# Attention on one Trainium2 core, summed by parts over differences of the values

## The chip, the cores and the metric

The kernel runs on one core of one Trainium2 chip. The metric is the device time of one execution in microseconds (us). Before the change it is 1481.43 us, the median of three runs (1478.18 to 1483.52). The profile describes a further execution, which took 1480.27 us.

## The reference

One decoder layer with three token mixers that read the same normalised input of 2048 tokens by 1024 columns. One combined projection feeds all three; their outputs are gated, joined and pass through one output projection. The change touches mixer C, stick-breaking attention with 6 heads of 64, for blocks of 128 queries:

```python
z = jnp.einsum('bthd,bshd->bhts', qb, kb) * scale
strict = s_idx[None, :] < t_idx[:, None]
log_not = jnp.where(strict, log_sigmoid(-z), 0.0)
suffix = lax.cumsum(log_not, axis=3, reverse=True) - log_not
a = jnp.where(strict, jnp.exp(log_sigmoid(z) + suffix), 0.0)
out = jnp.einsum('bhts,bshd->bthd', a, vb)
```

With b = sigmoid(z), the weight of key s is b(s) times the product of (1 - b) over all later allowed keys. Write S(s) for the product of (1 - b) over the keys s and later, a masked key counting 1. Then the weight is S(s+1) - S(s), and the sum over keys can be summed by parts: it is the last value row plus the sum over s of S(s) times (v(s-1) - v(s)), with v(-1) = 0.

## The kernel before, in words

Tokens stand in 16 tiles of 128, and these in three blocks of 5, 5 and 6 tiles (`BLOCKS`). Each block goes through three passes p = 0, 1, 2 of two heads each. A pass projects Q, K and V of its tiles (`c_proj`, and `c_evac` for what follows each tile's matmuls), then runs the attention (`stick`). While `stick` runs, `interleave` weaves in matmuls of the other projections as filler: three weight groups in passes 0 and 1, one in pass 2. After the third block a last part, from about 1213 us on, does the mLSTM and the output projection.

**Projection.** A group of weights fills 8 tiles of the pool `wr`, which holds 11. In block 0 the weights come from the input (`load_w`, line 168, into two `st` buffers), ScalarE casts them (line 189), VectorE or GpSimd takes the rest (line 190), and a store keeps both halves in DRAM (line 193); later blocks load those (line 183). In `c_evac`, ScalarE squares Q and K, VectorE sums (line 331), GpSimd takes the power -1/2 (lines 332 and 333), ScalarE and VectorE split V into a high and a low half in `Vst` (lines 334 and 335), and VectorE scales Q and K into `qk` (line 338), which TensorE transposes (line 344). Splits of one tile stand in the queues beside this chain.

**Attention.** A unit is one query tile, one head and up to four key tiles. `front` makes z with two matmuls (lines 378, 379), two sigmoids of z on ScalarE (383 into `bb`, 384 into `be`), on the diagonal two masks on GpSimd (386, 388), and a running product over `bb` from right to left on VectorE (391). One more column of `bb` holds 1 (a memset, line 382). Then `be` is multiplied by the shifted product, by VectorE in one unit and by GpSimd in the next:

```python
eng = nc.gpsimd if len(st_count) % 2 else nc.vector
eng.tensor_tensor(be[:, :w], be[:, :w], bb[:, 1:w + 1], ALU.mult)
```

`middle`, one unit later, transposes `be` (406) and splits the result (ScalarE 408, VectorE 409). `back`, another unit later, multiplies by `Vst` (421). `fin` adds the halves (437), copies (439, ScalarE) and stores `y_d` (440).

**Order.** The framework's scheduler decides the order on each engine from priorities (`prio`); each engine, and SyncE's queue (SP), which starts the DMAs, then takes its instructions in that order. A waiting instruction holds up all behind it.

Of the kernel before, what the change touches and what calls it, by code (L numbers as in the profile page):

```python
# [17 lines left out]
P = 128  # L18
# [14 lines left out]
def hybrid_block_kernel(ctx: ExitStack, tc: tile.TileContext, x, c, norm_g, w_ada, b_ada, w_in,  # L33
# [54 lines left out]

    lw = ExitStack()
    stg_p = lw.enter_context(tc.tile_pool(name="stg", bufs=2))  # L90
    wr_p = lw.enter_context(tc.tile_pool(name="wr", bufs=11))


    rs = ExitStack()
# [114 lines left out]
    brow = [stk.tile([P, 512], F32, tag="bb", bufs=4, name=f"brow{n}") for n in range(4)]  # L209
    for n in (2, 0, 3, 1):  # L210
        nc.gpsimd.memset(brow[n], 0.0)
    g_bc = [stk.tile([P, 512], F32, tag="be", bufs=3, name=f"g_bc{n}") for n in range(2)]

    def ada_load(half):
        for n, c0 in enumerate((1024 + 512 * half, 512 * half)):
# [86 lines left out]
    def c_proj(b, t0, nb, p):  # L302
# [17 lines left out]
            prev = nxt  # L320
        run(prev)

    def c_evac(b, t0, p, j, ps):
        i = t0 + j
        if p == 0:
            nc.vector.tensor_tensor(gates[:, :, i, :], ps[:, 384:392].rearrange("p (a h) -> p a h", a=2),
                                    bif_bc, ALU.add)
        sq = tmp.tile([P, 4, 64], F32, tag="sq", bufs=1, name=f"sq{p}_{i}")
        nc.scalar.activation(sq.rearrange("p a d -> p (a d)"), ps[:, 0:256], AF.Square)
        rr = tmp.tile([P, 4], F32, tag="rr", name=f"rr{p}_{i}")  # L330
        nc.vector.tensor_reduce(rr, sq, AX.X, ALU.add)
        nc.gpsimd.tensor_scalar(rr, rr, 1.0 / 64, EPS, ALU.mult, ALU.add)
        nc.gpsimd.tensor_tensor(rr, rr, neghalf[:, 0:4], ALU.pow)
        nc.scalar.copy(Vst[:, i, :, 0:64], ps[:, 256:384].rearrange("p (h d) -> p h d", h=2))
        nc.vector.tensor_tensor(Vst[:, i, :, 64:128], ps[:, 256:384].rearrange("p (h d) -> p h d", h=2),
                                Vst[:, i, :, 0:64].bitcast(F32), ALU.subtract)
# [12 lines left out]
        nc.vector.scalar_tensor_tensor(ks[64:128], pt[64:128, 2:4, :], gk[64:128], ks[64:128].bitcast(F32),  # L349
                                       ALU.mult, ALU.subtract)  # L350
        nc.vector.scalar_tensor_tensor(Qst[:, j, 1], pt[:, 0:2, :], gq, Qst[:, j, 0].bitcast(F32),  # L351
                                       ALU.mult, ALU.subtract)
        if b < len(BLOCKS) - 1:
            nc.sync.dma_start(k_d[p][:, :, i * P:(i + 1) * P], ks.bitcast(F32))
            nc.sync.dma_start(v_d[p][:, i], Vst[:, i].bitcast(F32))

    def stick(p, t0, nb):
        units = []
# [8 lines left out]
        acc = {}  # L367
        outs = {}
        st = {}
        st_count = []  # L370

        def front(u):
            i, j, h, s0, s1 = u
            w = (s1 - s0) * P
            nm = f"{p}_{i}_{h}_{s0}"
            z = pz.tile([P, 512], F32, tag="z", name=f"z{nm}")
            kk = Kst[:, h, s0 * P:s1 * P]
            nc.tensor.matmul(z[:, :w], lhsT=Qst[:, j, 0, h, :], rhs=kk, start=True, stop=False)  # L378
            nc.tensor.matmul(z[:, :w], lhsT=Qst[:, j, 1, h, :], rhs=kk, start=False, stop=True)  # L379
            bb = stk.tile([P, 513], F32, tag="bb", bufs=4, name=f"bb{nm}")  # L380
            be = stk.tile([P, 512], F32, tag="be", bufs=3, name=f"be{nm}")
            nc.gpsimd.memset(bb[:, w:w + 1], 1.0)  # L382
            nc.scalar.activation(bb[:, :w], z[:, :w], AF.Sigmoid, scale=-1.0)  # L383
            nc.scalar.activation(be[:, :w], z[:, :w], AF.Sigmoid)  # L384
            if s1 == i + 1:
                nc.gpsimd.affine_select(out=bb[:, w - P:w], in_=bb[:, w - P:w], pattern=[[-1, P]],  # L386
                                        compare_op=ALU.is_gt, fill=1.0, base=0, channel_multiplier=1)
                nc.gpsimd.affine_select(out=be[:, w - P:w], in_=be[:, w - P:w], pattern=[[-1, P]],
                                        compare_op=ALU.is_gt, fill=0.0, base=0, channel_multiplier=1)
            rev = bb[:, 0:w + 1][:, ::-1]  # L390
# [40 lines left out]
        def fin(u):  # L431
# [612 lines left out]
```

## Time and profile before

| what | value |
|---|---|
| median of three runs | 1481.43 us |
| the profiled execution | 1480.27 us |
| its span, first to last instruction | 1478.5 us |
| TensorE busy (matmuls) | 1400.6 us, 95% |
| VectorE (DVE) busy | 1025.1 us, 69% |
| ScalarE (ACT) busy | 678.1 us, 46% |
| GpSimd (POOL) busy | 647.3 us, 44% |
| mean granted TensorE clock | 0.982 |

Busy shares are averages over stages with different limits. The windows below give the same numbers by stretch: a stretch's length less TensorE's busy time is what TensorE stood idle there.

### The profile page before, as it was taken

How to read it: one execution, taken by the hardware profiler on the slowest of the kernel's cores; microseconds unless marked ns; L12 is line 12 of the kernel's file. 1: busy time of each engine (PE TensorE's matmuls, PEld its weight loads, DVE VectorE, ACT ScalarE, POOL GpSimd, SP SyncE). 2: the span in 40 equal slices, each digit the busy share in tenths (PEclk: the TensorE clock that was granted, in tenths of full speed). 3: DMA queues.
4: the chain of work that ended last, by engine and by line, in shares of the span. 5: the costliest groups of instructions: out<-in, count | busy, mean ns of one | idle time of the engine just before them, and what ended most of it. 6: DMA issues, size and time to landing. Idle time of an engine off the chain costs nothing.

```text
span 1478.5 us, 24942 instructions
## 1 busy us (share of the span) xinstructions
PE 1400.6 (95%) x8468; PEld 1302.7 (88%) x8468; DVE 1025.1 (69%) x1778; ACT 678.1 (46%) x1656; POOL 647.3 (44%) x1140
## 2 busy tenths in 40 slices
PE   4999999889999999999999899999999978999998
PEld 3789999879999999988899799989999867888887
DVE  6796555586894566588698975778778888444443
ACT  3365444444464355446367655555455655211210
POOL 4463554573443433455233353433344336534442
PEclk9999999999999999999999999999999998999999
DMA  9866766657635534625332343303432524555551
GB/s 319 305 203 216 249 213 190 207 187 240 203 114 194 175 114 137 213 98 184 114 117 78 104 148 131 104 27 107 158 100 74 190 89 128 185 152 159 171 156 57
DMA packets 187103, 233.19 MB, mean 158 GB/s; under 512 B 22714, under 2 KB 160344, under 8 KB 186976
## 3 DMA queue, kind: packets, MB, share of 16 engines
q1 hardware_dynamic: 186752, 231.59, 48.1%
q8 instruction: 67, 1.10, 0.3%
q14 instruction: 60, 0.49, 0.1%
q0 software_dynamic: 224, 0.02, 0.0%
HBM read 159.24 MB, written 72.31 MB: 157 GB/s over the span
## 4 chain that ended last, share of the span: by engine, by line
PE 68%; DVE 16%; DMA 5%; issue 4%; POOL 3%; ACT 3%; SPq 1%; DVEq 0%; POOLq 0%; ACTq 0%
DVE bb L391 6%; PE av L421 5%; PE pc L296 4%; PE pc L298 4%; PE at L406 4%; PE pc L297 4%; PE po L957 4%; PE po L959 3%; PE po L958 3%; PE pg L298 3%; PE pg L297 3%; PE pg L296 3%; PE pb L465 2%; PE pb L464 2%; PE z L378 2%
## 5 line engine op out<-in xcount | busy, mean ns | idle before, releaser
L391 DVE TENSOR_TENSOR_SCAN bb<-bb,bb 128x513 f32<-128x513 f32 x144 | 194.1, 1348 | 24.9 <-ACT bb L383 23.8
L395 POOL TENSOR_TENSOR be<-be,bb 128x512 f32<-128x512 f32 (+3 forms) x120 | 133.0, 1108 | 148.3 <-DVE bb L391 69.2
L409 DVE TENSOR_TENSOR aT<-at,aT 128x512 fp32r<-128x512 f32 (+3 forms) x240 | 142.7, 597 | 31.5 <-ACT aT L408 30.5
L421 PE MATMUL av<-aT,Vst 128*128 128x256 f32 x816 | 146.4, 296 | 15.0 <-DVE aT L409 12.1
L408 ACT CAST aT<-at 128x512 fp32r<-128x512 f32 (+3 forms) x240 | 127.1, 530 | 70.3 <-PE at L406 67.4
L383 ACT ACTIVATE bb<-z 128x512 f32<-128x512 f32 (+3 forms) x240 | 130.3, 544 | 54.5 <-PE z L379 44.2
L421 PEld LDWEIGHTS av<-aT,Vst 128*128 128x128 f32 x816 | 120.5, 192 | 27.0 <-DVE aT L409 19.2
L296 PE MATMUL pc<-wr,hT 128*128 128x384 f32 (+1 forms) x384 | 136.8, 358 | 7.6 <-DVE hT L290 5.7
L406 PE MATMUL at<-ident,be 128*128 128x128 f32 x816 | 132.8, 277 | 9.6 <-DVE Qst L351 4.5
L298 PE MATMUL pc<-wr,hT 128*128 128x384 f32 (+1 forms) x384 | 135.5, 353 | 1.6 <-DVE hT L290 1.5
L297 PE MATMUL pc<-wr,hT 128*128 128x384 f32 (+1 forms) x384 | 134.0, 349 | 0.0
L384 ACT ACTIVATE be<-z 128x512 f32<-128x512 f32 (+3 forms) x240 | 132.1, 550 | 0.0
L406 PEld LDWEIGHTS at<-ident,be 128*128 128x128 f32 x816 | 99.2, 142 | 19.0 <-DVE aT L409 8.0
L957 PE MATMUL po<-wo,yT 128*128 128x512 f32 x256 | 105.0, 410 | 0.3 <-ACT yT L946 0.3
L958 PE MATMUL po<-wo,yT 128*128 128x512 f32 x256 | 102.3, 400 | 1.9 <-DVE wo L864 1.9
L391 DVE TENSOR_TENSOR_SCAN bb<-bb 128x129 f32<-128x129 f32 (+3 forms) x96 | 86.9, 905 | 23.5 <-POOL bb L386 16.3
L959 PE MATMUL po<-wo,yT 128*128 128x512 f32 x256 | 101.5, 400 | 0.0
L382 POOL MEMSET bb<- 128x1 f32 x240 | 24.2, 101 | 168.4 <-DVE bb L391 118.1
L378 PE MATMUL z<-Kst,Qst 128*128 128x512 f32 (+3 forms) x240 | 92.7, 387 | 1.7 <-ACT be L384 1.6
L466 PE MATMUL pb<-hT,wr 128*128 128x320 f32 (+1 forms) x288 | 91.9, 324 | 2.4 <-DVE wr L190 2.4
L464 PE MATMUL pb<-hT,wr 128*128 128x320 f32 (+1 forms) x288 | 93.1, 324 | 0.6 <-DMA wr<-w_d 0.6
L465 PE MATMUL pb<-hT,wr 128*128 128x320 f32 (+1 forms) x288 | 92.2, 322 | 0.0
(272 smaller groups left out, 3905.2 us busy)
## 6 DMA issues: line engine op xcount, KB each, us to landing
wr<-w_d SPq DMA_DIRECT2D x160, 384.0 KB, 5.6
w_d<-wr SPq DMA_DIRECT2D x80, 384.0 KB, 3.5
wad<-in_w_ada_dram SPq DMA_DIRECT2D x8, 1024.0 KB, 6.8
xo<-in_x_dram SPq DMA_DIRECT2D x16, 512.0 KB, 3.7
out_dram<-o SPq DMA_DIRECT2D x31, 256.0 KB, 2.9
xt<-in_x_dram SPq DMA_DIRECT2D x15, 512.0 KB, 3.5
st<-in_w_in_dram SPq DMA_DIRECT2D x60, 128.0 KB, 3.7
wr<-w_d SPq DMA_DIRECT2D x16, 392.0 KB, 6.0
```

The lines of the kernel that those rows point to most:

```text
L296: nc.tensor.matmul(ps, lhsT=hT[:, 0, k, cols], rhs=wt[k][:, 0, :W], start=k == 0, stop=False)
L297: nc.tensor.matmul(ps, lhsT=hT[:, 0, k, cols], rhs=wt[k][:, 1, :W], start=False, stop=False)
L298: nc.tensor.matmul(ps, lhsT=hT[:, 1, k, cols], rhs=wt[k][:, 0, :W], start=False, stop=k == KT - 1)
L384: nc.scalar.activation(be[:, :w], z[:, :w], AF.Sigmoid)
L391: nc.vector.tensor_tensor_scan(rev, rev, rev, carry.get((i, h), 1.0), ALU.mult, ALU.bypass)
L395: eng.tensor_tensor(be[:, :w], be[:, :w], bb[:, 1:w + 1], ALU.mult)
L406: nc.tensor.transpose(at[:, s, :], be[:, s * P:(s + 1) * P], ident)
L409: nc.vector.tensor_tensor(aT[:, :nb_, 1, :], at[:, :nb_, :], aT[:, :nb_, 0, :].bitcast(F32), ALU.subtract)
L421: nc.tensor.matmul(flat(av), lhsT=Vst[:, s0 + s, h, :], rhs=flat(aT[:, s]), start=(s0 + s == i), stop=(s0 + s == 0))
L957: nc.tensor.matmul(po, lhsT=yT[:, 0, k, :], rhs=wo[k][:, 0, cs], start=k == 0, stop=False)
L958: nc.tensor.matmul(po, lhsT=yT[:, 0, k, :], rhs=wo[k][:, 1, cs], start=False, stop=False)
L959: nc.tensor.matmul(po, lhsT=yT[:, 1, k, :], rhs=wo[k][:, 0, cs], start=False, stop=k == KT - 1)
```

## The change

Summation by parts takes the second sigmoid, its mask, the memset and the multiplication out of `front`; `middle` transposes the running product `bb` itself. In exchange `Vst` holds differences v(s-1) - v(s), and `fin` adds the last value row.

For each token tile `c_evac` now copies V out of PSUM (`vt`, line 359), shifts it by one row with a DMA of 127 rows within SBUF (line 360), brings the first row from the tile before (line 357; a memset for the first tile of all) and stores the last row to DRAM (line 361). `values` makes the difference on GpSimd (line 333), its high half on ScalarE (336) and its low half on GpSimd (337), and stores it for later blocks (339). It is called two token tiles later, for the last two tiles of a pass out of `stick`. `stick` loads the last value row, repeated on all partitions (line 416), and VectorE adds it (line 463) where ScalarE copied. In these four places 189 DMAs are added: 45, 48, 48 and 48.

Beside it `bb` gets 6 buffers (4 of `bb` and 3 of `be` before), `wr` gets 13 tiles, and the DMA descriptor scratch of GpSimd is set to 4 KB.

```diff
-    wr_p = lw.enter_context(tc.tile_pool(name="wr", bufs=11))
+    wr_p = lw.enter_context(tc.tile_pool(name="wr", bufs=13))
...
+    def values(pool_after, act_after):
+        b, p, i, dv, vt = late.pop(0)
+        with tc.issue_after(pool_after.ins):
+            nc.gpsimd.tensor_tensor(dv, dv, vt, ALU.subtract)
+        dv2 = dv.rearrange("p (h d) -> p h d", h=2)
+        with tc.issue_after(act_after.ins):
+            nc.scalar.copy(Vst[:, i, :, 0:64], dv2)
+        nc.gpsimd.tensor_tensor(Vst[:, i, :, 64:128], dv2, Vst[:, i, :, 0:64].bitcast(F32), ALU.subtract)
+        if b < len(BLOCKS) - 1:
+            nc.sync.dma_start(v_d[p][:, i], Vst[:, i].bitcast(F32))
...
-        nc.gpsimd.tensor_tensor(rr, rr, neghalf[:, 0:4], ALU.pow)
-        nc.scalar.copy(Vst[:, i, :, 0:64], ps[:, 256:384].rearrange("p (h d) -> p h d", h=2))
-        nc.vector.tensor_tensor(Vst[:, i, :, 64:128], ps[:, 256:384].rearrange("p (h d) -> p h d", h=2),
-                                Vst[:, i, :, 0:64].bitcast(F32), ALU.subtract)
+        rr_pow = nc.gpsimd.tensor_tensor(rr, rr, neghalf[:, 0:4], ALU.pow)
+        dv = tmp.tile([P, P], F32, tag="dv", bufs=4, name=f"dv{p}_{i}")
+        if i == 0:
+            nc.gpsimd.memset(dv[0:1, :], 0.0)
+        else:
+            nc.sync.dma_start(dv[0:1, :], v_before[p][P - 1:P, :])
+        vt = vt_end[:, p, :] if j == BLOCKS[b] - 1 else tmp.tile([P, P], F32, tag="vt", bufs=4, name=f"vt{p}_{i}")
+        v_copy = nc.scalar.copy(vt, ps[:, 256:384])
+        nc.sync.dma_start(dv[1:P, :], vt[0:P - 1, :])
+        nc.sync.dma_start(vl_d[p * NT + i:p * NT + i + 1, :], vt[P - 1:P, :])
+        v_before[p] = vt
+        late.append((b, p, i, dv, vt))
+        if j >= 2:
+            values(rr_pow, v_copy)
...
-            bb = stk.tile([P, 513], F32, tag="bb", bufs=4, name=f"bb{nm}")
-            be = stk.tile([P, 512], F32, tag="be", bufs=3, name=f"be{nm}")
-            nc.gpsimd.memset(bb[:, w:w + 1], 1.0)
-            nc.scalar.activation(bb[:, :w], z[:, :w], AF.Sigmoid, scale=-1.0)
-            nc.scalar.activation(be[:, :w], z[:, :w], AF.Sigmoid)
+            bb = stk.tile([P, 512], F32, tag="bb", bufs=BB, name=f"bb{nm}")
+            front_act[0] = nc.scalar.activation(bb[:, :w], z[:, :w], AF.Sigmoid, scale=-1.0)
...
-                nc.gpsimd.affine_select(out=be[:, w - P:w], in_=be[:, w - P:w], pattern=[[-1, P]],
-                                        compare_op=ALU.is_gt, fill=0.0, base=0, channel_multiplier=1)
-            rev = bb[:, 0:w + 1][:, ::-1]
+                if h == 0:
+                    vlast[i] = stk.tile([P, P], F32, tag="vlast", name=f"vlast{p}_{i}")
+                    nc.sync.dma_start(vlast[i], vl_d[p * NT + i:p * NT + i + 1, :].broadcast_to([P, P]))
+            rev = bb[:, 0:w][:, ::-1]
...
-            eng.tensor_tensor(be[:, :w], be[:, :w], bb[:, 1:w + 1], ALU.mult)
...
-                nc.tensor.transpose(at[:, s, :], be[:, s * P:(s + 1) * P], ident)
+                nc.tensor.transpose(at[:, s, :], bb[:, s * P:(s + 1) * P], ident)
...
-            nc.scalar.copy(yc, py[:, 0:P])
+            nc.vector.tensor_tensor(yc, py[:, 0:P], vlast.pop(i), ALU.add)
...
+            if late and n >= 2:
+                values(front_pool[0], front_act[0])
...
-    nc = _bacc.Bacc("TRN2", target_bir_lowering=False, num_devices=1)
+    nc = _bacc.Bacc("TRN2", target_bir_lowering=False, num_devices=1, dynamic_dma_scratch_size=4096)
```

How the order moves, at three places. First VectorE in the last attention pass (block 2, p = 2), at query tile 15; the running product is printed as SCALAR_TENSOR_TENSOR, and a name holds pass, tile, head and first key tile. Before:

```order
L391 SCALAR_TENSOR_TENSOR bb2_15_0_12_14287<-bb2_15_0_12_14287 128x513
L395 TENSOR_TENSOR be2_15_0_12_14288<-be2_15_0_12_14288,bb2_15_0_12_14287 128x512
L391 SCALAR_TENSOR_TENSOR bb2_15_0_8_14316<-bb2_15_0_8_14316,bb2_15_0_12_14287 128x513
L409 TENSOR_TENSOR aT2_14_1_4_14274<-at2_14_1_4_14269,aT2_14_1_4_14274 128x4x128
L391 SCALAR_TENSOR_TENSOR bb2_15_0_4_14345<-bb2_15_0_4_14345,bb2_15_0_8_14316 128x513
L409 TENSOR_TENSOR aT2_14_1_0_14303<-at2_14_1_0_14298,aT2_14_1_0_14303 128x4x128
L395 TENSOR_TENSOR be2_15_0_4_14346<-be2_15_0_4_14346,bb2_15_0_4_14345 128x512
L391 SCALAR_TENSOR_TENSOR bb2_15_0_0_14394<-bb2_15_0_0_14394,bb2_15_0_4_14345 128x513
```

and of the change:

```order
L418 SCALAR_TENSOR_TENSOR bb2_15_0_12_13688<-bb2_15_0_12_13688 128x512
L433 TENSOR_TENSOR aT2_14_0_0_13609<-at2_14_0_0_13604,aT2_14_0_0_13609 128x4x128
L418 SCALAR_TENSOR_TENSOR bb2_15_0_8_13714<-bb2_15_0_8_13714,bb2_15_0_12_13688 128x512
L433 TENSOR_TENSOR aT2_14_1_12_13629<-at2_14_1_12_13625,aT2_14_1_12_13629 128x3x128
L418 SCALAR_TENSOR_TENSOR bb2_15_0_4_13739<-bb2_15_0_4_13739,bb2_15_0_8_13714 128x512
L451 TENSOR_TENSOR avt2_14_0_13638<-av2_14_0_13544,avs2_14_0_13636 128x128
L433 TENSOR_TENSOR aT2_14_1_8_13654<-at2_14_1_8_13649,aT2_14_1_8_13654 128x4x128
L418 SCALAR_TENSOR_TENSOR bb2_15_0_0_13784<-bb2_15_0_0_13784,bb2_15_0_4_13739 128x512
L433 TENSOR_TENSOR aT2_14_1_4_13675<-at2_14_1_4_13670,aT2_14_1_4_13675 128x4x128
```

The multiplications between the products are gone, and the products run further ahead: those of tile 15 now stand among the splits of tile 14's first head.

Second SP in block 0, at the projection of p = 2; `st10` and `wr10` are that projection's weights, `w_d` the stores. Before:

```order
L168 DMA st10_0_3400<-in_w_in_dram 128x2x128 x3
L440 DMA y_d_63<-yc1_4_3043 128x128
L193 DMA w_d2952_6_3131<-wr9_3_0_3128 256x1x384
L193 DMA w_d2952_7_3136<-wr9_3_1_3133 256x1x384
L193 DMA w_d128_0_3407<-wr10_0_0_3404 256x1x384
L168 DMA st10_1_3414<-in_w_in_dram 128x2x128
L193 DMA w_d128_1_3412<-wr10_0_1_3409 256x1x384
L168 DMA st10_1_3414<-in_w_in_dram 128x2x128 x2
L168 DMA st10_2_3428<-in_w_in_dram 128x2x128 x3
L563 DMA y_d_63<-gu0_0_2782 128x5x64 x2
L355 DMA v_d2_73<-Vst_444 128x256 x2
L193 DMA w_d128_2_3421<-wr10_1_0_3418 256x1x384
```

and of the change:

```order
L171 DMA st10_0_3397<-in_w_in_dram 128x2x128 x2
L171 DMA st10_1_3411<-in_w_in_dram 128x2x128 x3
L464 DMA y_d_63<-yc1_4_3017 128x128
L196 DMA w_d128_0_3404<-wr10_0_0_3401 256x1x384
L360 DMA dv2_0_3143<-vt2_0_3145 127x128
L196 DMA w_d128_1_3409<-wr10_0_1_3406 256x1x384
L196 DMA w_d128_2_3418<-wr10_1_0_3415 256x1x384
L171 DMA st10_2_3425<-in_w_in_dram 128x2x128 x2
L196 DMA w_d128_3_3423<-wr10_1_1_3420 256x1x384
L171 DMA st10_2_3425<-in_w_in_dram 128x2x128
L171 DMA st10_3_3439<-in_w_in_dram 128x2x128 x3
L589 DMA y_d_63<-gu0_0_2765 128x5x64 x2
```

The loads of `st10` follow each other sooner, and the last of them stand ahead of the stores of V and K; the shift of tile 0 (line 360) stands between stores of weights.

Third GpSimd at the same projection (`rr` is the scale of Q and K by tile). Before:

```order
L332 TENSOR_SCALAR rr2_1_3200<-rr2_1_3200 128x4
L333 TENSOR_TENSOR rr2_1_3200<-rr2_1_3200,neghalf_81 128x4
L332 TENSOR_SCALAR rr2_2_3246<-rr2_2_3246 128x4
L333 TENSOR_TENSOR rr2_2_3246<-rr2_2_3246,neghalf_81 128x4
L190 TENSOR_TENSOR wr10_1_1_3423<-st10_1_3414,wr10_1_1_3423 128x384
L332 TENSOR_SCALAR rr2_3_3292<-rr2_3_3292 128x4
L333 TENSOR_TENSOR rr2_3_3292<-rr2_3_3292,neghalf_81 128x4
L190 TENSOR_TENSOR wr10_2_1_3437<-st10_2_3428,wr10_2_1_3437 128x384
```

and of the change:

```order
L350 TENSOR_SCALAR rr2_1_3178<-rr2_1_3178 128x4
L351 TENSOR_TENSOR rr2_1_3178<-rr2_1_3178,neghalf_82 128x4
L350 TENSOR_SCALAR rr2_2_3227<-rr2_2_3227 128x4
L351 TENSOR_TENSOR rr2_2_3227<-rr2_2_3227,neghalf_82 128x4
L333 TENSOR_TENSOR dv2_0_3143<-dv2_0_3143,vt2_0_3145 128x128
L337 TENSOR_TENSOR Vst_446<-dv2_0_3143,Vst_446 128x2x64
L350 TENSOR_SCALAR rr2_3_3280<-rr2_3_3280 128x4
L193 TENSOR_TENSOR wr10_2_1_3434<-st10_2_3425,wr10_2_1_3434 128x384
L351 TENSOR_TENSOR rr2_3_3280<-rr2_3_3280,neghalf_82 128x4
L333 TENSOR_TENSOR dv2_1_3182<-dv2_1_3182,vt2_1_3184 128x128
L193 TENSOR_TENSOR wr10_3_1_3448<-st10_3_3439,wr10_3_1_3448 128x384
L337 TENSOR_TENSOR Vst_446<-dv2_1_3182,Vst_446 128x2x64
```

The difference of tile 0 stands behind the power of tile 2 and ahead of that of tile 3, that of tile 1 directly behind tile 3's.

## Rows read from the trace of the kernel before

**Rows 1.** Page, part 4: chain that ended last, by engine, by line.

```profile
PE 68%; DVE 16%; DMA 5%; issue 4%; POOL 3%; ACT 3%; SPq 1%; DVEq 0%; POOLq 0%; ACTq 0%
DVE bb L391 6%; PE av L421 5%; PE pc L296 4%; PE pc L298 4%; PE at L406 4%; PE pc L297 4%; PE po L957 4%; PE po L959 3%; PE po L958 3%; PE pg L298 3%; PE pg L297 3%; PE pg L296 3%; PE pb L465 2%; PE pb L464 2%; PE z L378 2%
```

**Rows 2.** Windows: length, PE, PEld, DVE, ACT, POOL, clock, DMA share, GB/s.

```profile
0.00:60.00 60.00, 38.08 (x145) 27.04 (x146) 41.35 (x64) 17.71 (x36) 27.42 (x47) 0.91 0.86 300
60.00:120.00 60.00, 57.08 (x387) 54.96 (x386) 52.38 (x102) 36.87 (x100) 34.81 (x69) 1.00 0.73 245
...
240.00:304.00 64.00, 55.21 (x301) 52.45 (x300) 38.09 (x77) 26.29 (x80) 34.77 (x53) 0.91 0.59 184
304.00:420.00 116.00, 112.75 (x711) 107.35 (x710) 92.84 (x174) 58.75 (x155) 54.71 (x107) 0.99 0.66 216
420.00:620.00 200.00, 199.99 (x1254) 193.64 (x1253) 124.54 (x234) 91.61 (x233) 68.87 (x152) 1.00 0.46 151
620.00:712.00 92.00, 82.67 (x509) 78.22 (x508) 78.30 (x119) 51.86 (x130) 55.13 (x95) 0.97 0.43 141
...
810.00:850.00 40.00, 34.48 (x211) 29.99 (x210) 37.49 (x61) 27.16 (x58) 14.97 (x33) 1.00 0.29 96
...
960.00:1050.00 90.00, 87.87 (x562) 83.28 (x561) 74.25 (x120) 48.31 (x118) 33.18 (x72) 1.00 0.25 83
...
1110.00:1175.00 65.00, 63.56 (x406) 59.29 (x404) 51.25 (x81) 40.81 (x97) 24.17 (x61) 1.00 0.29 103
1175.00:1213.00 38.00, 27.38 (x167) 22.60 (x166) 34.60 (x43) 22.48 (x47) 14.63 (x27) 0.91 0.38 137
1213.00:1260.00 47.00, 41.07 (x243) 35.74 (x244) 36.62 (x60) 21.09 (x50) 29.10 (x29) 0.85 0.51 154
...
sum 1478.50, PE 1400.59 PEld 1302.72 DVE 1025.14 ACT 678.15 POOL 647.32; mean PE 87.54 PEld 81.42 DVE 64.07 ACT 42.38 POOL 40.46
```

**Rows 3.** Groups by line and shape: count, busy us, mean ns, idle before.

```profile
L391 DVE TENSOR_TENSOR_SCAN bb<-bb,bb 128x513 f32<-128x513 f32 x144 | 194.1, 1348 | 24.9 <-ACT bb L383 23.8
...
L395 DVE TENSOR_TENSOR be<-be,bb 128x512 f32<-128x512 f32 x66 | 51.1, 774 | 1.3
...
L544 POOL TENSOR_TENSOR gu<-tb 128x128 f32<-128x128 f32 x32 | 20.0, 626 | 29.5 <-DVE tb L543 28.6 <-PE at L406 0.8
...
L335 DVE TENSOR_TENSOR Vst<-pc,Vst 128x128 fp32r<-128x128 f32 x48 | 13.3, 280 | 3.5 <-ACT Vst L334 3.5
...
L384 ACT ACTIVATE be<-z 128x512 f32<-128x512 f32 (+3 forms) x240 | 132.1, 550 | 0.0
```

**Rows 4.** Busy time by stretch, line 395 alone: DVE, then POOL.

```profile
810.00:850.00 40.00, 3.65 (x6) 9.79 (x7) 1.00 0.29 96
...
1175.00:1213.00 38.00, 5.47 (x7) 10.20 (x8) 0.91 0.38 137
...
sum 1478.50, DVE 77.44 POOL 133.01; mean DVE 4.84 POOL 8.31
```

**Rows 5.** Timeline, 626 to 634 us, DVE, POOL: start, length.

```profile
627.13 2.37 DVE L395 TENSOR_TENSOR be<-be,bb 128x256 f32<-128x256 f32 x1
629.42 3.40 DVE L391 TENSOR_TENSOR_SCAN bb<-bb,bb 128x513 f32<-128x513 f32 x1
...
626.46 5.29 POOL L149 TENSOR_TENSOR xt<-xt,hshift 128x1024 f32<-128x1024 f32 x2
```

**Rows 6.** Chain by time, 250 to 304 us: start, length, what.

```profile
264.35 3.42 DMA st<-in_w_in_dram
...
267.87 0.52 ACT wr L189
```

**Rows 7.** SP waits (total, times, longest); DMA issues; line 355.

```profile
SPq L310 <- PE av L421: 44.6, 8, 14.6
...
v_d<-Vst SPq DMA_DIRECT2D x30, 128.0 KB, 3.7
...
L355 SPq DMA_DIRECT2D v_d<-Vst x30: 319/378/1351, 60.4 to 620.2; - x30
```

More of the change, by code (lines that the diff above doesn't have):

```diff
@@ L27 @@
 T5 = 6
+BB = 6
 OFF = dict(au=0, av=256, az=512, bq=768, bk=1152, bv=1536, bo=1920, bz=2304, bi=2688,
@@ L53, in hybrid_block_kernel @@
     v_d = [dram.tile([P, NT, 2, P], F32, name=f"v_d{p}") for p in range(3)]
+    vl_d = dram.tile([3 * NT, P], F32, name="vl_d")
     ident = const.tile([P, P], F32, name="ident")
@@ L75, in hybrid_block_kernel @@
     gates = const.tile([P, 2, NT, 4], F32, name="gates")
+    vt_end = const.tile([P, 3, P], F32, name="vt_end")
     gT = const.tile([P, 64], F32, name="gT")
@@ L208, in hybrid_block_kernel @@
     crow = tmp.tile([8, P], F32, tag="t512", bufs=T5, name="crow")
-    brow = [stk.tile([P, 512], F32, tag="bb", bufs=4, name=f"brow{n}") for n in range(4)]
+    brow = [stk.tile([P, 512], F32, tag="bb", bufs=BB, name=f"brow{n}") for n in range(4)]
     for n in (2, 0, 3, 1):
         nc.gpsimd.memset(brow[n], 0.0)
-    g_bc = [stk.tile([P, 512], F32, tag="be", bufs=3, name=f"g_bc{n}") for n in range(2)]
+    g_bc = [stk.tile([P, 512], F32, tag="bb", bufs=BB, name=f"g_bc{n}") for n in range(2)]
     def ada_load(half):
@@ L321, in c_proj @@
         run(prev)
+    late = []
+    v_before = {}
+    def values(pool_after, act_after):
[8 more added lines that the diff above has]
+            nc.sync.dma_start(v_d[p][:, i], Vst[:, i].bitcast(F32))
     def c_evac(b, t0, p, j, ps):
@@ L354, in c_evac @@
             nc.sync.dma_start(k_d[p][:, :, i * P:(i + 1) * P], ks.bitcast(F32))
-            nc.sync.dma_start(v_d[p][:, i], Vst[:, i].bitcast(F32))
     def stick(p, t0, nb):
@@ L369, in stick @@
         st = {}
-        st_count = []
+        vlast = {}
+        front_act, front_pool = [None], [None]
         def front(u):
@@ L379, in front @@
             nc.tensor.matmul(z[:, :w], lhsT=Qst[:, j, 1, h, :], rhs=kk, start=False, stop=True)
-            bb = stk.tile([P, 513], F32, tag="bb", bufs=4, name=f"bb{nm}")
-            be = stk.tile([P, 512], F32, tag="be", bufs=3, name=f"be{nm}")
-            nc.gpsimd.memset(bb[:, w:w + 1], 1.0)
-            nc.scalar.activation(bb[:, :w], z[:, :w], AF.Sigmoid, scale=-1.0)
-            nc.scalar.activation(be[:, :w], z[:, :w], AF.Sigmoid)
+            bb = stk.tile([P, 512], F32, tag="bb", bufs=BB, name=f"bb{nm}")
+            front_act[0] = nc.scalar.activation(bb[:, :w], z[:, :w], AF.Sigmoid, scale=-1.0)
             if s1 == i + 1:
-                nc.gpsimd.affine_select(out=bb[:, w - P:w], in_=bb[:, w - P:w], pattern=[[-1, P]],
+                front_pool[0] = nc.gpsimd.affine_select(out=bb[:, w - P:w], in_=bb[:, w - P:w], pattern=[[-1, P]],
                                         compare_op=ALU.is_gt, fill=1.0, base=0, channel_multiplier=1)
-                nc.gpsimd.affine_select(out=be[:, w - P:w], in_=be[:, w - P:w], pattern=[[-1, P]],
-                                        compare_op=ALU.is_gt, fill=0.0, base=0, channel_multiplier=1)
-            rev = bb[:, 0:w + 1][:, ::-1]
+                if h == 0:
+                    vlast[i] = stk.tile([P, P], F32, tag="vlast", name=f"vlast{p}_{i}")
+                    nc.sync.dma_start(vlast[i], vl_d[p * NT + i:p * NT + i + 1, :].broadcast_to([P, P]))
+            rev = bb[:, 0:w][:, ::-1]
             nc.vector.tensor_tensor_scan(rev, rev, rev, carry.get((i, h), 1.0), ALU.mult, ALU.bypass)
             carry[i, h] = bb[:, 0:1]
-            eng = nc.gpsimd if len(st_count) % 2 else nc.vector
-            st_count.append(0)
-            eng.tensor_tensor(be[:, :w], be[:, :w], bb[:, 1:w + 1], ALU.mult)
-            st[u] = [be, None]
+            st[u] = [bb, None]
             return 2 * w / 2.4
@@ L401, in middle @@
             nm = f"{p}_{i}_{h}_{s0}"
-            be = st[u][0]
+            bb = st[u][0]
             nb_ = s1 - s0
```

## The prediction

> **What bounds the kernel now.** I read the chain of work that ended last first. TensorE has 68% of it, VectorE 16%, and the running product of line 391 is its longest single line [rows 1]. The change removes no matmul and no transpose, so TensorE's 1400.6 us of work stay [rows 2], and what can be won is the time in which it stands idle or runs at the lower clock. So I cut the span into windows next [rows 2]. Idle is length less TensorE's busy time. From 420 to 620 us it is 0.01 us of 200: there nothing can be won, however much other engines are relieved. Idle worth the name is found in 60 to 120 (2.92), 240 to 304 (8.79), 304 to 420 (3.25), 620 to 712 (9.33), 810 to 850 (5.52), 960 to 1050 (2.13), 1110 to 1175 (1.44) and 1175 to 1213 (10.62): 44.0 us in eight stretches. The start (21.92) and the passage to the last part (5.93) hold no attention that the change touches.
>
> In the same rows the reader sees why. In 810 to 850 VectorE is busy 37.49 of 40 us, in 1175 to 1213 it is 34.60 of 38: there it sets the pace, and line 391 and its followers are its work. In 240 to 304 it is busy only 38.09 of 64, and the chain there runs through a weight load of 3.42 us and the cast behind it [rows 6]: a different cause. [...]
>
> **The change part by part.** ScalarE loses the second sigmoid, 240 of them, 132.1 us at 550 ns [rows 3]. ScalarE paces no stretch (678 us in all [rows 2]), so I count only that each product starts one sigmoid earlier, at nothing: TensorE's filler hides it, and without the filler it would be 0.55 us where a pass begins. GpSimd loses 133.0 us of multiplications, VectorE 77.4 us [rows 4]. The mask and the memset go from GpSimd's queue as well. VectorE's split of V, 13.3 us [rows 3], moves to GpSimd, and 48 additions in `fin` come to VectorE at about the same size, so these two cancel there. GpSimd gains 96 subtractions of 128 by 128; the nearest row has 626 ns [rows 3], 60 us in all, under what it loses. By stretch:
>
> - 1175 to 1213, the last pass. The 5.47 us of multiplications on VectorE fall out of the queue that sets the pace [rows 4]; the order shows products and splits alternating with nothing between. I take 5.5 of the idle 10.62, and half of the clock's 3.4 with it: 7.2. Ends: 0, if TensorE then waits for the products alone, and 14.0.
> - 810 to 850: 3.65 us of multiplications [rows 4], taken whole: 3.7. Ends 0 and 5.52.
> - 960 to 1050 and 1110 to 1175: idle 3.57 together, VectorE busy four fifths of the time [rows 2]. I take 2.5; ends 0 and 3.57.
> - 620 to 712: a multiplication of only 256 columns took 2.37 us and the product behind it 3.40 us, while GpSimd ran two additions of 1024 columns, 5.29 us [rows 5]; the mean product takes 1.35 and a full multiplication 0.77 [rows 3]. The multiplication goes, GpSimd's additions stay. I take 5.0 of the idle 9.33 and the clock's 2.8. Ends 0 and 12.1.
> - 240 to 304: the two more weight tiles let loads of the third projection start sooner, as SP's order shows, but a load still has to land and its split still stands ahead of `qk`. I take 2.5; ends 0 and 14.6 (8.79 and 5.8).
> - 304 to 420: 1.5, ends 0 and 4.5. From 60 to 120: 1.0, ends 0 and 2.9, since there the DMA engines are 73% busy [rows 2] and SP gets 14 more issues.
>
> Sum: 7.2 + 3.7 + 2.5 + 5.0 + 2.5 + 1.5 + 1.0 = 23.4 us. All upper ends give 57.2.
>
> [...]
>
> [...]
>
> Against the gain stand the added waits. 189 DMAs at the 0.378 us that an issue of line 355 takes [rows 7] are 71 us of SP's time over the whole kernel. I cost them at nothing: SP is no compute engine, and between the shift and the difference lie two tiles of projection. One tile is 24 matmuls, at 200 us for 1254 matmuls [rows 2] 3.8 us, so two are 7.7; a 128 KB store of V lands in 3.7 us in the median [rows 7], and the shift moves half of that. The cover is gone where SP holds the shift back: then GpSimd waits at the difference, behind it the power of the next tile, on VectorE `qk`, and TensorE waits for the transposed Q and K. [...]
>
> The sum is made against the profiled execution: 1480.27 - 23.4 = 1456.9 us. The median of the runs is 1.2 us above that execution, so I forecast **1458 us** for the change.
>
> **The rivals.** *Larger gain.* Once VectorE keeps up, the waits at pass starts shrink too, the clock stays up, and products no longer collide. For it: four stretches show both idle and lost clock. Against it: weight and x loads remain. About three quarters of the upper ends, 43 us: 1481.4 - 43 = 1438 us.
>
> *Smaller gain.* Only the stretches that VectorE paces answer: 7.2 + 3.7 + 2.5 = 13.4, so 1468 us. For it: the chain at 264 us runs through a load.
>
> *No change.* TensorE is 95% busy and its waits pass to other work that was nearly as late, the splits (line 409) and the x loads: 1479 us.
>
> *Slower.* SP's queue holds the shifts back. Before, the loads of `Vst` already waited there for the last attention matmul 8 times, 44.6 us in all and 14.6 us at the longest [rows 7], and in later blocks the shifts stand behind such loads. A mean wait of 5.6 plus 3.7 us of landing is 9.3, 1.6 beyond the cover of 7.7; the longest is 18.3, 10.6 beyond. If four of the nine projections meet the longest, that is 42 us, less 23.4 won: 19 us slower, 1500 us. It decides from a mean excess of 28 / 9 = 3.1 us per projection on. Against it: the first differences stand two tiles late, and the wait for attention's last matmul is largely over by the third tile.
>
> *The change doesn't do what it says* would be differences built late enough that `back` waits for `Vst`. The tiles left over are two and are read last, so I give it no chance of its own; it is in the slower case.
>
> **How the numbers follow.** Chances: the forecast 0.42, larger 0.19, smaller 0.16, no change 0.09, slower 0.14. A measurement of this kernel can tell about 0.3%, 4.4 us, from no change: faster is below 1477.0, slower above 1485.9. Faster is 0.42 + 0.19 + 0.16 = 0.77, same 0.09, slower 0.14. The range reaches from 1432, a little past the larger gain (below it lie the all-upper-ends cases near 1424), to 1480, through no change; about 0.05 is left out below and 0.14 above.
>
> **What would show it.** Right: VectorE's total near 948 us (1025 less 77), ScalarE's near 546 (678 less 132), GpSimd's below 575 (647 less 133, and 60 more); the last pass shorter by 7 us, with VectorE no longer ahead of 0.9 busy; line 418 with a smaller share of the chain than line 391; TensorE's busy time within a few us of 1400, and 420 to 620 unchanged but for its place. Wrong: GpSimd waiting in total over 20 us at line 333 for DMAs, `qk` (now line 367) waiting more for GpSimd, and TensorE idle before the transposes of line 373. If idle of the last pass stays near 10 us although VectorE is relieved, the product's own chain was the limit and the sum falls by its largest term. If 240 to 304 and 620 to 712 lose most of their idle, the larger gain is the case.

## The result and the profile after

The change makes the kernel slower: 1514.02 us in the median (1510.92 to 1515.98, 4 runs) against 1481.91 us for the kernel before (1478.18 to 1483.52, 4 runs), a ratio of 1.0223 with a 95% interval of 1.0203 to 1.0243. The forecast was 1458 us, and 1514 lies above the range.

The arithmetic went down as intended, and TensorE did not gain by it. The page of the kernel after, busy time by engine and the chain:

```profile
PE 1412.6 (93%) x8468; PEld 1314.6 (87%) x8468; DVE 941.8 (62%) x1658; ACT 577.9 (38%) x1416; POOL 504.4 (33%) x783
...
PE 61%; DMA 15%; DVE 9%; issue 5%; SPq 4%; ACT 3%; POOL 3%; DVEq 0%; POOLq 0%; ACTq 0%
...
L418 DVE TENSOR_TENSOR_SCAN bb<-bb,bb 128x512 f32<-128x512 f32 x144 | 190.4, 1322 | 14.9 <-ACT bb L410 13.4
```

VectorE lost 83 us, ScalarE 100, GpSimd 143. In the chain VectorE fell from 16% to 9%, but DMA rose from 5% to 15% and SP's queue from 1% to 4% [rows 1]: more of the span now hangs on transfers. The windows show where. Kernel after, columns as in [rows 2]; the last row is the whole middle part, from 60 us to the last attention matmul:

```profile
60.00:120.00 60.00, 53.23 (x332) 50.26 (x331) 39.51 (x78) 29.50 (x82) 27.46 (x51) 0.95 0.69 225
120.00:250.00 130.00, 124.02 (x752) 120.20 (x751) 66.67 (x132) 53.38 (x140) 50.85 (x83) 0.99 0.71 224
250.00:330.00 80.00, 68.70 (x381) 66.00 (x380) 47.25 (x91) 31.80 (x96) 42.48 (x63) 0.94 0.61 186
330.00:380.00 50.00, 45.83 (x283) 43.63 (x282) 30.74 (x68) 20.75 (x55) 19.52 (x30) 0.97 0.59 198
380.00:440.00 60.00, 50.08 (x284) 48.12 (x283) 36.52 (x66) 19.47 (x53) 17.23 (x32) 0.89 0.59 188
...
851.00:891.00 40.00, 38.44 (x247) 36.49 (x246) 32.34 (x56) 21.30 (x45) 2.54 (x8) 1.00 0.29 98
...
1211.00:1249.00 38.00, 31.23 (x206) 26.18 (x205) 32.62 (x43) 20.01 (x41) 4.76 (x5) 0.96 0.65 228
...
60.00:1249.20 1189.20, 1121.95 (x6925) 1073.41 (x6924) 762.36 (x1355) 507.58 (x1258) 356.88 (x615) 0.98 0.48 154
```

The same stretch of the kernel before:

```profile
60.00:1213.40 1153.40, 1108.76 (x6907) 1059.76 (x6906) 848.45 (x1472) 606.72 (x1494) 499.35 (x968) 0.99 0.47 153
```

Length less busy time is TensorE's idle: 44.6 us before, 67.3 after. Its busy time grew by 13.2 us with the same matmuls at a lower mean clock, and 22.6 + 13.2 is the 35.8 us by which the span grew. From 60 to 440 us stand 6.8, 6.0, 11.3, 4.2 and 9.9 us of idle, 38.1 in all; from 60 to 420 us before it was 15.3. The late stretches that VectorE paced did gain: 851 to 891 has 1.6 us idle where 810 to 850 had 5.5, and the last 38 us have 6.8 where they had 10.6. So a gain late is buried under a loss early, at the projections. What the engines waited for there, kernel after (engine, line, what ended the wait: us in total, times, longest):

```profile
ACT wr L192 <- DMA st<-in_w_in_dram: 78.7, 28, 9.1
ACT Vst L336 <- POOL dv L333: 67.4, 25, 8.4
POOL dv L333 <- DMA dv<-vt_end: 36.4, 7, 8.0
POOL dv L333 <- DMA dv<-vt: 13.2, 6, 6.1
...
SPq L312 <- PE z L408: 29.9, 6, 13.4
...
PE z L407 <- ACT bb L410: 15.4, 8, 5.3
```

The first row was 50.9 us (22 times) before; the next three are new. The last row is where TensorE feels them most: its matmuls of z wait for a sigmoid in ScalarE's queue, in four of the eight cases one shortly behind a wait of the first two rows. Before, TensorE waited 1.6 us there. And this is SP's queue of the kernel after at the first shifts (start us, length us):

```profile
63.55 0.73 SPq L360 DMA_DIRECT2D dv<-vt  x1
64.34 3.46 SPq L361 DMA_DIRECT2D vl_d<-vt  x1
67.85 0.62 SPq L357 DMA_DIRECT2D dv<-vt  x1
68.58 0.64 SPq L360 DMA_DIRECT2D dv<-vt  x1
69.27 1.94 SPq L361 DMA_DIRECT2D vl_d<-vt  x1
```

The issue that takes long is the 512 bytes of line 361, right behind the shift of line 360. By tile, kernel after (duration min/median/max in ns):

```profile
L361 SPq DMA_DIRECT2D vl_d<-vt x39: 294/1017/5145, 64.3 to 1125.7; - x39
L361 SPq DMA_DIRECT2D vl_d<-vt_end x9: 1467/2665/4782, 90.9 to 1127.9; - x9
...
L360 SPq DMA_DIRECT2D dv<-vt x39: 625/655/727, 63.6 to 1119.2; - x39
```

Summed over all its issue records, SP spends 601 us on 1012 issues, 417 us on 823 before; 80 us of it are the 48 issues of line 361.

### The profile page after: what moved, and what is told of

It is laid out like the page before. It is cut to its first block, busy times and chain, and to the rows that moved or that the text cites. A ratio compares the mean times of both kernels' runs of the same rounds, so it can differ in the third digit from the quotient of the medians.

```text
span 1514.3 us, 24153 instructions
## 1 busy us (share of the span) xinstructions
PE 1412.6 (93%) x8468; PEld 1314.6 (87%) x8468; DVE 941.8 (62%) x1658; ACT 577.9 (38%) x1416; POOL 504.4 (33%) x783
## 4 chain that ended last, share of the span: by engine, by line
PE 61%; DMA 15%; DVE 9%; issue 5%; SPq 4%; ACT 3%; POOL 3%; DVEq 0%; POOLq 0%; ACTq 0%
PE av L445 5%; PE at L430 4%; DMA st<-in_w_in_dram 4%; PE po L983 4%; PE po L985 4%; PE po L984 4%; PE pc L299 3%; PE pc L300 3%; PE pc L301 3%; DVE bb L418 3%; DMA wr<-w_d 3%; DMA dv<-vt_end 2%; PE z L407 2%; PE z L408 2%; PE pg L299 2%
## 5 line engine op out<-in xcount | busy, mean ns | idle before, releaser
L418 DVE TENSOR_TENSOR_SCAN bb<-bb,bb 128x512 f32<-128x512 f32 x144 | 190.4, 1322 | 14.9 <-ACT bb L410 13.4
L430 PE MATMUL at<-ident,bb 128*128 128x128 f32 x816 | 133.0, 278 | 7.5 <-DVE Qst L380 4.0
L430 PEld LDWEIGHTS at<-ident,bb 128*128 128x128 f32 x816 | 100.7, 143 | 15.9 <-DVE aT L433 4.4
L407 PE MATMUL z<-Kst,Qst 128*128 128x512 f32 (+3 forms) x240 | 93.5, 392 | 15.4 <-ACT bb L410 15.4
L412 POOL TENSOR_SCALAR_AFFINE_SELECT bb<-bb 128x128 f32<-128x128 f32 x96 | 40.4, 422 | 179.5 <-ACT bb L410 149.9
L418 DVE TENSOR_TENSOR_SCAN bb<-bb 128x128 f32<-128x128 f32 (+3 forms) x96 | 83.3, 869 | 25.0 <-POOL bb L412 24.4
L490 PE MATMUL pb<-hT,wr 128*128 128x320 f32 (+1 forms) x288 | 95.5, 332 | 2.6 <-ACT wr L192 2.4
L299 PE MATMUL pa<-wr,hT 128*128 128x384 f32 x256 | 90.3, 353 | 6.9 <-DMA wr<-w_d 4.1
L491 PE MATMUL pb<-hT,wr 128*128 128x320 f32 (+1 forms) x288 | 94.4, 328 | 0.0
L492 PE MATMUL pb<-hT,wr 128*128 128x320 f32 (+1 forms) x288 | 94.4, 330 | 0.0
L299 PE MATMUL pg<-wr,hT 128*128 128x384 f32 x256 | 90.0, 351 | 2.4 <-DMA wr<-w_d 2.4
```

Of the source, the lines that this page charges most:

```text
L299: nc.tensor.matmul(ps, lhsT=hT[:, 0, k, cols], rhs=wt[k][:, 0, :W], start=k == 0, stop=False)
L430: nc.tensor.transpose(at[:, s, :], bb[:, s * P:(s + 1) * P], ident)
```

## The experiments

Three theories. **A**: SP's time for the added issues is the loss. **B**: it is the waiting for the shift's landing, in the order of GpSimd and ScalarE. **C**: the 13 weight tiles. **D** came up after the first four runs and is told there.

**The last value row without its DMAs.** 96 DMAs less; instead of adding the row, 1 is subtracted where the weights are split.

```diff
-        nc.sync.dma_start(vl_d[p * NT + i:p * NT + i + 1, :], vt[P - 1:P, :])
-            nc.scalar.copy(aT[:, :nb_, 0, :], at[:, :nb_, :])
+            nc.scalar.activation(aT[:, :nb_, 0, :], at[:, :nb_, :], AF.Copy, bias=-1.0)
```

> The last value row is no longer stored, loaded and added (96 DMAs less): since the differences telescope, the weights S - 1 give the same sum, and ScalarE and VectorE take the 1 off where they split the transposed product. Theory A (SyncE's queue is filled by the issue of the added DMAs, 159 us of issue time in the profile after, 101 us of it lines 361 and 416, and weight loads behind them come late): most of the 32 us loss comes back, 1485 to 1497 us. Theory B (the engines wait in order for the shift to land): the shift stays, so 1507 to 1515 us. Theory C (the other buffer counts gave a worse order): 1507 to 1515 us.

Measured: 1494.09 us, ratio 1.01 (1.0084 to 1.0117). Some 18 to 20 us come back (by the ratios and by the medians), as A had it. But the long issue only moved to the next in line. Line 357, which now follows the shift of the tile before, takes 66.5 us in 45 issues; in the changed kernel it took 26.7.

**The shifts on ScalarE's queue.** Lines 357, 360 and 361 with `nc.scalar.dma_start`.

> The shift, the first row and the store of the last row (lines 360, 357, 361; 138 us of issue time) are issued by ScalarE, right behind its copy of V, instead of SyncE; the load of the last row stays on SyncE. Theory A: SyncE is as free as before, 1482 to 1495 us, unless ScalarE's 138 us of issuing take the place. Theory B: the landing time is the same, 1505 to 1515 us. Theory C: 1505 to 1515 us.

Measured: 1515.92 us, ratio 1.0245 (1.0229 to 1.0262): nothing gained, though SP's issue time is back at 431 us. That alone does not refute A, which left open that ScalarE's issuing takes the place: ScalarE now spends 135 us on 141 issues. The run has another use: these DMAs now have a queue of their own in the records, q10, beside SP's q1. A stretch in which hardly anything else moves, 199.5 to 202.2 us (DMA busy tenths and GB/s in 40 slices; then packets, MB, share of 16 engines' time by queue):

```profile
DMA  0000000000000000000000000000000000000002
GB/s 23 15 23 23 23 23 23 23 23 23 23 23 23 23 23 23 23 23 23 15 23 23 23 23 23 23 23 15 23 23 23 23 15 23 23 23 23 23 23 91
...
q10 hardware_dynamic: 84, 0.04, 5.2%
q1 hardware_dynamic: 29, 0.02, 2.4%
```

The 23 GB/s are the rate of both queues together, and it hardly changes whether q10 moves alone (12 to 25 GB/s by slices from 93.5 to 94.4 us) or takes turns with q1: one packet of 512 B after the other, about 24 ns apart (113 in 2.7 us). Together the queues take 7.6% of sixteen engines' time here. One sixteenth is 6.25%; the records give a little more because a packet's record, by these rows 27 ns on q10 and 36 on q1, lasts longer than the 24 ns to the next. So 127 packets are 3 us at this pace, while in the first 60 us of the kernel before the DMA engines together move 300 GB/s [rows 2].

The single packets of this stretch show what stands behind the shift. SP had issued a store of V at 196.17 us and one of K at 196.60. Fifteen sixteenths of each, 120 of 128 packets and 240 of 256, had started by 198.5 us. The last 8 of V started between 199.92 and 200.38 us and the last 16 of K between 200.90 and 201.60, each in turn with a packet of the shift, while nothing else moved.

**Without the shift.** Lines 357 and 360 are left out and `dv` is minus `vt`, so the row above is missing from the values; the store and load of the last row stay.

```diff
-        nc.sync.dma_start(dv[1:P, :], vt[0:P - 1, :])
-            nc.gpsimd.tensor_tensor(dv, dv, vt, ALU.subtract)
+            nc.gpsimd.tensor_tensor(dv, vt_zero, vt, ALU.subtract)
```

> The two shift DMAs (lines 360 and 357, 93 of them, 58 us of issue time) are left out and the difference is taken from a tile of zeros, so the attention's values are wrong by the row before; the rest of the change stays. Theory A: about a third of the loss comes back, 1498 to 1506 us. Theory B (waiting for the shift is the loss): nearly all, 1480 to 1492 us. Theory C: 1507 to 1515 us.

Measured: 1451.39 us, ratio 0.9815 (0.98 to 0.983). All of the loss is gone and the gain is there. The run takes away the wait for the landing too, so by itself it tells only that the shift is the cause, not how. The row that tells most is line 362 of this kernel, the same store of 512 B with no shift ahead of it:

```profile
L362 SPq DMA_DIRECT2D vl_d<-vt x39: 215/247/730, 61.1 to 1058.2; - x39
```

247 ns in the median in the place of 1017: the small store was never dear, it was held up by what stood before it.

**11 weight tiles.** `bufs=11` for `wr`, all else as changed.

> The change with 11 weight tiles as before instead of 13. Theories A and B: no better, 1510 to 1525 us, since fewer loads run ahead. Theory C (13 tiles let weight loads stand too early in SyncE's queue and hold up what is behind them): 1480 to 1500 us.

Measured: 1506.46 us, ratio 1.0185 (1.0169 to 1.0201). The two tiles cost 6 to 8 us here (by the ratios and by the medians), so C is a small part at most; the time lies outside the ranges of all three theories.

From these four came **theory D**: the 127 rows run on one DMA engine, and whatever is spread over all engines, the weight loads above all, stands behind them there. It is read from the records of the run on ScalarE's queue: the 23 GB/s in 7.6% of sixteen engines' time, the packets of the two queues in turn, the last sixteenth of each store among them, and the time, 1515.92 us, which the other queue did not change. No record names the engine that moves a packet, so the one engine is the author's estimate from that pace.

**The shift in two pieces**, of 112 and 15 rows.

```diff
-        nc.sync.dma_start(dv[1:P, :], vt[0:P - 1, :])
+        nc.sync.dma_start(dv[1:113, :], vt[0:112, :])
+        nc.sync.dma_start(dv[113:P, :], vt[112:P - 1, :])
```

> Edit: the shift of 127 rows is issued as two, rows 1 to 112 and rows 113 to 127; all else is the changed kernel, and each token tile issues one DMA more (48 more in all). In the run with the shifts on ScalarE's queue, that queue alone moved data from 93.5 to about 96.5 us: 130 packets, 5.7 to 7.0% of sixteen engines' time, at 19 to 25 GB/s, so one packet of 512 B after the other. Theory D: the shift of 127 rows runs on one DMA engine, and what is split over all engines (weights, the next store) waits behind it there; 112 and 15 rows are divided over more engines, so the time falls to 1455 to 1480 us and the mean issue of the last row's store falls from 1.7 us to under 0.6. Theory A (SP's issue time is the loss, whatever the DMA's shape): 48 more issues at about 0.6 us are added to a full queue, 1515 to 1540 us. Theory B (the loss is waiting for a landing in POOL's and ScalarE's order, whatever sets it): falls by what the landing shortens, 1475 to 1505. [...]

Measured: 1465.58 us, ratio 0.99 (0.9881 to 0.992), 48 us less than the changed kernel with 48 issues more. The rows behind it, of this kernel:

```profile
L362 SPq DMA_DIRECT2D vl_d<-vt x39: 253/403/827, 65.6 to 1077.8; - x39
```

D's figures hold: the time, and a mean issue of 0.39 us for the last row's store. A as it was written is refuted, and B's range began 9 us higher. How the 112 and the 15 rows divide over the engines is not shown. One statement in the expectation is not right: q10 was not alone from 93.5 to 96.5 us, where q1 moved 307 packets beside its 119.

**Through DRAM.** The tile's 128 rows are stored one row down and loaded back as 128 rows.

```diff
+        nc.sync.dma_start(vs_d[p, i * P + 1:i * P + P + 1, :], vt)
...
+            nc.sync.dma_start(dv, vs_d[p, i * P:i * P + P, :])
```

> Edit: each tile's 128 value rows are stored to DRAM one row down and loaded back as 128 rows; the row from the tile before and the last row's store fall away, and the last row is read from the same place. About 144 added DMAs in the place of 189, none of them of 127 rows (but for the three first tiles, which keep the shift on the chip, split in 112 and 15). Theory D (127 rows on one DMA engine): both copies are spread, 1455 to 1480 us. Theory A (SP's issue time): 45 issues less, some 90 us of issue less, 1480 to 1500. Theory B (waiting for landings in order): two landings one behind the other in the place of one, 1515 us or more.

Measured: 1460.92 us, ratio 0.9867 (0.9845 to 0.9888). With two landings in series, of 128 rows each, the kernel is faster than with the one of 127 rows (1514.02 us), which B excludes. Its windows and waits:

```profile
60.00:1190.00 1130.00, 1095.26 (x6915) 1052.58 (x6914) 763.15 (x1355) 506.93 (x1258) 360.18 (x615) 1.00 0.51 165
...
1152.00:1190.00 38.00, 31.35 (x216) 26.25 (x215) 32.41 (x44) 20.59 (x42) 6.45 (x5) 1.00 0.65 229
```

```profile
ACT wr L192 <- DMA st<-in_w_in_dram: 62.5, 28, 9.1
ACT Vst L336 <- POOL dv L333: 35.1, 24, 3.8
POOL dv L333 <- DMA dv<-vs_d: 16.3, 10, 5.1
```

Against the kernel before, idle of the middle part is down from 44.6 to 34.7 us and busy time by 13.5, at a clock of 1.00: 23.4 us shorter. The tail takes 2.2 us more; why was not looked into.

**The weight as a difference**, on the kernel before: `be` is the difference of neighbouring elements of `bb`; second sigmoid, mask and product go, no DMA comes.

```diff
-            eng.tensor_tensor(be[:, :w], be[:, :w], bb[:, 1:w + 1], ALU.mult)
+            eng.tensor_tensor(be[:, :w], bb[:, 1:w + 1], bb[:, :w], ALU.subtract)
```

> Edit, on the kernel before: the attention weight is formed as the difference of two neighbouring elements of the scan's output, in the place of the second sigmoid, its mask and the product; values, weight tiles and DMAs stay as before. One 512-wide ScalarE operation and one mask less per unit, no DMA more. If ScalarE's share in the passes is what the changed kernel saves, 1455 to 1472 us; if the saving lies mainly in the product that falls off VectorE and GpSimd, which stays here as a difference, 1472 to 1482 us (no change).

Measured: 1492.88 us, ratio 1.0078 (1.0059 to 1.0097), a miss: slower, though ScalarE does 98 us less. In this kernel the tile's waits read:

```profile
  PE at L403: 79.4, 52
```

In the kernel before the same wait, for the transposes that still read a `be` buffer, was 17.0 us in 3 waits. It seems to have stood in ScalarE's queue and now to stand in those of VectorE and GpSimd, ahead of the next products; that was not tried by itself. Taking the second sigmoid and its mask alone gains nothing.

**No added DMA at all**: the first and the third experiment together, so values are negated in the place of differenced, and the row above is missing from them.

> Edit: the changed kernel without any of the 189 added DMAs: values are negated in the place of differenced, and 1 is subtracted from the weights in the place of adding the last value row. It shows the gain of the change's arithmetic alone. Theory D: the store and load of the last row cost little by themselves (0.28 us an issue where no shift stands before them), so within 8 us of the run without the shifts, 1443 to 1453 us. Theory A: 96 DMAs less again, another 20 us less, 1425 to 1435 us.

Measured: 1450.49 us, ratio 0.9794 (0.9772 to 0.9815). This is the gain of the arithmetic together with the change's buffers, which stay (six of `bb`, 13 weight tiles; not tried apart from it): 29.6 us against the runs of before beside it. It is 0.9 us (by the medians) to 3 us (by the ratios) from the run without shifts that still has the 96 DMAs of the last row: those cost 3 us at most by themselves, and some 18 to 20 us behind a shift.

**127 idle rows on the kernel before.** One more DMA for each token tile into a spare tile that nothing reads, ahead of the store of V.

```diff
+        sp = tmp.tile([P, P], F32, tag="sp", bufs=2, name=f"sp{p}_{i}")
+        nc.sync.dma_start(sp[1:P, :], Vst[0:127, i, 0, :].bitcast(F32))
```

> Edit, on the kernel before: each of the 48 token tiles issues one more DMA, 127 rows of 512 B from the stored values into a spare tile one row down, which nothing reads. No arithmetic changes and nobody waits for it. Theory D (127 rows run on one DMA engine and hold up what is split over all of them): 48 such transfers of about 3.3 us stand in front of weight loads, slower by 15 to 45 us. Theory B (the loss is that GpSimd and ScalarE wait for the landing): 0 to 5 us. Theory A (issue time): 48 issues of 0.65 us, 0 to 8 us, and the same for 128 rows.

Measured: 1514.4 us, ratio 1.0234 (1.0211 to 1.0257). No arithmetic changed, and the kernel is as slow as the changed one. No compute engine waits for these transfers. SP does, for a spare buffer to come free, but only 7.1 us in two waits (2.9 with the 128 rows of the next run).

**128 idle rows**, the control: `sp[0:P]` from `Vst[0:128]`.

> The control of the run with 127 idle rows: the same 48 idle DMAs on the kernel before, of 128 rows (no row shift). Theory D: within 6 us of the kernel before, 1474 to 1486 us. Theory A: as slow as with 127 rows.

Measured: 1481.14 us, ratio 1.0004 (0.9991 to 1.0017). One row more takes the whole loss away. The two runs differ in the offset of one row as well, but the split shift has that offset too and is fast. The store of V that stands behind the idle DMA, by tile, with 127 rows:

```profile
L357 SPq DMA_DIRECT2D v_d<-Vst x30: 415/2222/4291, 62.9 to 646.4; - x30
```

and with 128:

```profile
L357 SPq DMA_DIRECT2D v_d<-Vst x30: 320/587/1229, 62.4 to 621.6; - x30
```

The wait of the weights' cast for its load, with 127 rows:

```profile
ACT wr L189 <- DMA st<-in_w_in_dram: 69.8, 27, 7.9
```

and with 128, where it is about that of the kernel before, 50.9:

```profile
ACT wr L189 <- DMA st<-in_w_in_dram: 52.5, 21, 6.5
```

So both signs of the changed kernel, the long issue behind the shift and the late weights, are there with 127 rows and gone with 128. Summed over all its issues SP spends 528 us with 127 rows and 445 with 128. Theory D stands, its one engine as an estimate; A and B each name only a part. How the 33 us divide between SP's longer issues and the later landings was not separated.

**Through DRAM with 11 weight tiles.**

> Edit: the kernel that carries the values through DRAM, with 11 weight tiles as before the change. In the changed kernel 11 tiles were 8 us faster than 13. If that came from weight loads crowding the one engine that the shifts took, it is gone here: within 4 us of 1461. If 13 tiles cost by themselves, 1450 to 1456 us.

Measured: 1467.24 us, ratio 0.9906 (0.9886 to 0.9926), outside both expectations: 13 tiles are 6 us faster here, where they were 6 to 8 us slower with the shifts. The sign turns with the shifts, though the intervals with and without the two tiles just touch here; that earlier weight loads crowd the one engine is the likely reason, but was argued, not shown.

**Through DRAM, and 1 subtracted from the weights.** The edits of the first and sixth experiment together.

> Edit: the kernel that carries the values through DRAM, and with 1 subtracted from the weights where they are split, in the place of loading and adding the last value row: 48 DMAs less, none of them of an odd shape, and the copy of the output back on ScalarE. Candidate for the fastest. If the 48 loads cost what their issue takes (0.42 us each, in part in the open), 1452 to 1459 us; if spread DMAs are hidden, 1458 to 1464.

Measured: 1459.94 us, ratio 0.9865 (0.9842 to 0.9888), the same as through DRAM alone, 1460.92: the 48 loads of the last row cost nothing here that could be measured. These two versions beat the kernel before by 19 and 22 us, and the changed one by some 53.

## Why the prediction was wrong

**The step that failed** is the one on the added waits: "189 DMAs at the 0.378 us that an issue of line 355 takes ... I cost them at nothing", with "a 128 KB store of V lands in 3.7 us in the median, and the shift moves half of that". It priced the shift by its bytes and by a row of 128 partitions. The 127 rows had another price: on ScalarE's queue they moved at 23 GB/s, with what took turns with them in 7.6% of sixteen engines' time, about that of one engine. With the shift through DRAM or in two pieces the change measured 1461 and 1466 us, near the forecast, in the place of 1514: the term put at nothing was worth about 50 us. The step also counted only what waits for the shift. The 127 idle rows show that such a wait is not needed: 33 us are lost though no compute engine waits for them, while the next issue on SP stands up to 4.3 us and the weights' cast waits 69.8 us for its loads in the place of 52.5.

**The wait at the difference** is likely a second cost. GpSimd waited 49.6 us at line 333, over the 20 us named as a sign of error, and ScalarE 67.4 us behind it (24.7 us without the shifts). The cover of 7.7 us did not suffice where a landing was itself queued: single waits reach 8.0 us. Between the changed kernel and the one with the split shift lie 48 us, more than the 33 of the idle rows. TensorE's wait for the sigmoid, 15.4 us in the changed kernel, is 5.9 with the split shift, 0.6 without the shifts and 4.3 with the idle rows. That fits, but how much of the rest is this wait was not separated.

**The slower rival** had the right sign and place of wait ("SP's queue holds the shifts back", 1500 us) and the wrong mechanism. It expected the loads of `Vst` to hold the shifts back. But SP's waits at the loads of `Kst` and `Vst` fell: 75.1 us before, 44.6 of them the longest row [rows 7], and 51.8 after, 29.9 of them the row of line 312 above. And 25 us of the loss are there by the end of the first block (its last attention matmul starts at 374.5 us, 349.5 before), where no such load exists. The shifts held back the others. Nor did the path run through `qk`: VectorE's wait there for the power is 32.0 us, 28.7 before.

**The sum of the gain came out near**, once no DMA of 127 rows was left, and in part by luck. Predicted 23.4 us; the version through DRAM gains 19.2 by its runs, 23.4 in the middle part of its profiled execution, and the kernel without added DMAs 29.6. The predicted 23.4 was for the most part idle time; of the measured 23.4 idle gave 9.9, and 13.5 came from busy time at the higher clock (1.00 in the place of 0.99). Of the totals named as signs, VectorE's (941.8 us) and GpSimd's (504.4) came. ScalarE's is 577.9 in the place of 546: the records of its instructions overlap (in the kernel before they add up to 801 us, in 678 us of busy time), so a group's time does not come off the total whole. By terms:

- The last pass, predicted 7.2: 4.0 us of idle (10.62 to 6.65 for 38 us, taken from its end) and 3.4 of clock (1.00 in the place of 0.91) through DRAM, 7.4. In the changed kernel 3.9 of idle and 1.9 of clock (0.96).
- 810 to 850, predicted 3.7: 4.0 us even in the changed kernel.
- 620 to 712, predicted 5.0: through DRAM the same stretch has 3.9 us idle in the place of 9.3, and its clock is 1.00 in the place of 0.97, the 2.8 us.
- 240 to 304, predicted 2.5: through DRAM none of the idle came back (11.8 us from 240 to 320, 8.8 before), though the clock there rose from 0.91 to 0.98. Without any added DMA the stretch has 5.7 us idle, so a gain of that size is there when SP has nothing added.
- The clock: its terms (3.4 and 2.8 us, in upper ends also 5.8 and 1.2) are estimates, a stretch's length times what its clock in [rows 2] lacks to 1.00, 13.2 us in the four stretches. No run shows such a term by itself. What the runs show is TensorE's busy time in the middle part: 13.5 us less through DRAM, at a clock of 1.00 in the place of 0.99, and 13.2 us more in the changed kernel, at 0.98. I counted only a part: half of the 3.4, and what the 5.0 in 620 to 712 holds of the 2.8.

**Products that collide with GpSimd's work**, a part of the larger gain, are read from one pair: 2.37 and 3.40 us on VectorE while GpSimd added [rows 5]. With 120 multiplications gone from GpSimd the full product went from 1348 to 1322 ns, 2%, 3.7 us in all, so little was to be had there.

## What to carry to other kernels

Price a DMA by a run with its own number of rows, not by its bytes: a shift by one row makes 127 of 128 rows, and 48 such copies, which nothing in the kernel uses, cost the kernel before 33 us, where 48 of 128 rows cost nothing that could be measured. Here it helped to cut the copy into 112 and 15 rows (1465.58 us in the place of 1514.02) or to let it pass through DRAM as 128 rows (1460.92). For a DMA that is added to a full queue, ask what stands behind it, not only who waits for it; one idle transfer per tile, with a control of another shape, measures that without touching the arithmetic.

## What was not expected of the hardware

The slow DMA of 127 rows is seen first in the issue time of the next, unrelated DMA: 1017 ns in the median for 512 B behind it, 247 ns without it, up to 5145 ns at worst. On which engine the issuing is done made no difference here (1515.92 against 1514.02 us): on ScalarE's queue the same line still took up to 3278 ns. And here a single row made the price: 128 rows cost nothing that could be measured (1481.14 us), 127 cost 33 us (1514.4).
